# Latent queries by channels for all tokens, later loads of norm constants and residual rows, and other steps for the conditioning map's rows

## Chip, cores and metric

The kernel runs on one core of a Trainium2 chip. The metric is the device time of one execution in microseconds, as the median of several executions. Engines are named as the profile names them: PE (matmul) with PEld (its weight loads), DVE (vector), ACT (scalar), POOL (GpSimd) and SP (the queue that issues most DMAs).

## The reference, cut to what matters

Two layers run over 384 tokens, which are 128 context tokens (block 0) and 256 latent tokens (blocks 1 and 2). Each layer has four token mixers on one combined input projection, a gated merge, an output product with a normalisation, and then an MLP with a second normalisation. All weights and inputs are fp32.

```python
def _layer(x, cond, lp, mixer_fn):
    mod = jax.nn.silu(cond) @ lp['w_ada'] + lp['b_ada']
    sh1, sc1, g1, sh2, sc2, g2 = jnp.split(mod[:, None, :], 6, axis=-1)
    y, extra = mixer_fn(x * (1 + sc1) + sh1)
    x = _layernorm(ALPHA * x + g1 * y, lp['ln1_g'], lp['ln1_b'])
    h = x * (1 + sc2) + sh2
    f = jnp.square(jax.nn.relu(h @ lp['w_up'])) @ lp['w_down']
    x = _layernorm(ALPHA * x + g2 * f, lp['ln2_g'], lp['ln2_b'])
...
    qa = (_rmsnorm(q_lat, lp['mla_q_norm']) @ lp['mla_w_uq']).reshape(b, t, MLA_HEADS, MLA_NOPE + MLA_ROPE)
    return dict(
        a_q_nope=qa[..., :MLA_NOPE], a_q_pe=qa[..., MLA_NOPE:],
        a_ckv=_rmsnorm(kv_lat, lp['mla_kv_norm']), a_k_pe=k_pe,
...
    q_pe = _apply_rope(p['a_q_pe'], cos_a, sin_a)
    k_pe = _apply_rope(p['a_k_pe'][:, :, None, :], cos_a, sin_a)[:, :, 0]
...
    terms = [jax.nn.sigmoid(gates[..., i * D_MODEL:(i + 1) * D_MODEL]) * (o @ lp['w_branch'][i])
             for i, o in enumerate(outs)]
    return (terms[0] + terms[1] + terms[2] + terms[3]) @ lp['w_o']
```

Branch A is latent attention with four heads of 64 channels without position and 32 with position (its query latents have 256 channels). Branch B is retention with a norm per head, C is windowed attention, D is dense attention.

## The kernel before, in words

**Products.** Each fp32 weight tile of 128x1024 is split in two parts that PE can multiply at its fast rate: ACT copies the high part (L283), DVE subtracts for the low part (`split_low`, L127), and every product is three matmuls (`mm3`, L122 to L124). `Stream` holds the order of all weight tiles, loads up to four ahead into a ring of six raw buffers (`raw_load`, L274, on SP's queue) and splits two ahead.

**Order of a layer's first half.** The projection writes the mixers' inputs by token (`tm[key, t]`). After each block of a projection or a gate product the kernel calls `tick()`, which takes one more task into the `Pipe` and runs one stage of every task in it. Layer 0 has 16 ticks in the projections and 32 in the gates (two for each pair of gate columns), layer 1 has 22 and 32. Then `tick()` runs rows of the conditioning map: a call of the generator `ada_vector` is one DVE operation over 128x1024 (L378), and the rows' weights come through the same ring of raw buffers. How many calls a tick makes stands in `TICK_OPS` as pairs of a first tick and a number n; a tick makes n/2 calls, rounded up at odd ticks and down at even ones. Once the attention's buffers are given back (`p2` is set, ahead of the last branch's gates) n is 2. What is left is run by `for _ in ada_v: pass` ahead of the output product. Layer 0 has 48 calls, layer 1 has 32.

**Latent queries (branch A).** `prep_a(t)` makes three stages for each of three token blocks. `norms` takes sums of squares (L790, L791), the inverse root on POOL, two transposes of the query latents (L799) and a DVE copy of them (L800). `up_q` multiplies them with the up weights (L819, output by token, 384 columns, plain fp32), scales by the norm (L824), turns the position keys, and rotates the positional part of the queries on POOL and DVE. `turn` transposes each head's 96 channels back (L837, four transposes for a block) and copies them to `qTA` (L838). `keys_a` and `values_a` follow as tasks of their own, so branch A has five tasks ahead of its attention.

**Retention's norm.** `out_b(t)` has four stages: products, `norm`, `apply` (four DVE operations over 128x64, L1086, and one over 128x256, L1088) and `turn` (two transposes, L1096).

**Output product and normalisation.** `out_product` multiplies 8 (mixer) or 32 (MLP) weight tiles into six PSUM banks, all tokens at once for the first part (`lead`), and then the last `rest` tiles block by block, so that a block's normalisation (`layer_norm`) runs under the next block's matmuls. `raw` multiplies by the gate (L1250), adds the residual (L1251) and takes statistics (L1254). The very last block of the kernel has its second half cut into two pieces of 256 columns. The banks of the output product are those that the branch products used, so its first matmuls wait for the merge (`mid_done`, L1192).

**Late constants.** The norm constants (gate rows from DRAM and the norm's gain and bias, `norm_consts`, L1225, on POOL's queue) and the three residual blocks (`xs`, L1438, on SP's queue) are asked for ahead of the output product. A scheduler orders each engine's instructions by the program's order and its own estimate of when they are ready, so that these loads may move ahead of their place; `behind(later, earlier)` pins one instruction after another in that order.

Of the kernel before, what the change touches and what calls it, by code (L numbers as in the profile page):

```python
# [20 lines left out]
L = 2  # L21
# [20 lines left out]
TICK_OPS = ((4, 2), (14, 1), (29, 4))  # L42
# [53 lines left out]
def kernel(ctx, tc, a):  # L96
# [14 lines left out]
    def nm(s):  # L111
        counter[0] += 1
        return f"{s}_{counter[0]}"
# [157 lines left out]

    def raw_load(src, pool=None, bufs=RAWS):
        raw = raw_tile(src.shape[-1], pool, bufs)
        nc.sync.dma_start(out=raw, in_=src)  # L274
        return raw
# [190 lines left out]
    for l in range(L):  # L466
# [315 lines left out]
        def prep_a(t):  # L782
            st_ = {}
            tok = slice(t * P, (t + 1) * P)
            rs = rsa[:, t]

            def norms():
                x = tm["a", t]
                sq = t2("sq")
                nc.scalar.activation(sq[:, 0:256], x[:, 0:256], AF.Square, accum_out=rs[:, 0:1])  # L790
                nc.scalar.activation(sq[:, 256:384], x[:, 256:384], AF.Square, accum_out=rs[:, 1:2])  # L791
                nc.vector.tensor_scalar(out=rs[:, 0:1], in0=rs[:, 0:1], scalar1=1.0 / 256, scalar2=EPS, op0=ALU.mult,
                                        op1=ALU.add)
                nc.vector.tensor_scalar(out=rs[:, 1:2], in0=rs[:, 1:2], scalar1=1.0 / 128, scalar2=EPS, op0=ALU.mult,
                                        op1=ALU.add)
# [9 lines left out]
                if t == 0:  # L805
                    nc.sync.dma_start(out=a["o_ckv"][0, l], in_=kv)
                    nc.sync.dma_start(out=a["o_kpe"][0, l], in_=x[:, 384:416])
                    st_["pe"] = x[:, 384:416]
                else:
# [3 lines left out]
                    st_["pe"] = r.rearrange("p h s f -> p (h s f)")  # L813

            def up_q():
                qlT = st_["qlT"]
                qb = bank(psa)
# [3 lines left out]
                nc.tensor.transpose(tb[:, 0:P], tm["a", t][:, 256:384], ident)  # L821
# [284 lines left out]
        for t in range(3):  # L1106
            pipe.add(*prep_a(t))
# [616 lines left out]
```

## Time and profile before

| | |
|---|---|
| median of 3 runs | 1275.6 us (1275.33 to 1277.57) |
| the profiled execution | 1278.41 us, of which 1276.3 us are its span |
| busy | PE 1255.7 us, PEld 1140.0, DVE 852.7, ACT 583.5, POOL 214.5 |
| granted TensorE clock, mean | 0.996 |

The span runs from the first to the last instruction. All rows have times from the span's start. Matmuls overlap, so a row's duration is longer than the step from one matmul's start to the next one's; the step is what a matmul costs. A row of a window gives the stretch, its length, the busy time (and instructions) of PE, PEld, DVE, ACT and POOL, PE's granted clock, the DMA engines' mean busy share and GB/s. An entry such as [2.39 <-DVE tt L1192] says that the engine was idle for 2.39 us and what ended it.

### The profile page before, as it was taken

Reading aid. Unit: us, or ns where it says so; the run is one execution under the profiler, and the core shown is the slowest. Engines: PE = TensorE matmul, PEld = TensorE weight load, DVE = VectorE, ACT = ScalarE, POOL = GpSimd, SP = SyncE. Lnnn points to the kernel's source line nnn. Section 1 sums busy time; section 2 is a strip of 40 time slices with the busy share of each in tenths; the row PEclk is TensorE's granted clock in tenths of the full one; section 3 lists DMA queues with packets and bytes.
Section 4 is the critical chain, followed back from the end, with each engine's and each line's share of the span. In section 5 each row is a group of like instructions: output and inputs, shape, how many; then the busy total and the mean of one; then the engine's idle time right before and its main releaser. Section 6 shows DMA issues by size and latency. Waiting matters only on the chain. (4 is left out here: it accounts for less than half of the span.)

```text
span 1276.3 us, 19137 instructions
## 1 busy us (share of the span) xinstructions
PE 1255.7 (98%) x7264; PEld 1140.0 (89%) x7264; DVE 852.7 (67%) x1537; ACT 583.5 (46%) x1054; POOL 214.5 (17%) x218
## 2 busy tenths in 40 slices
PE   9999999999999999999999999999999999999996
PEld 7889888999889999999898988999998999999995
DVE  4676965899679999443486876597456893333345
ACT  4654563333446444454365566233343744444451
POOL 0032200333232000000061210024221500000004
PEclk9999999999999999999999999999999999999998
DMA  9843323469626787454324422348344263334421
GB/s 371 335 153 118 124 87 104 145 207 348 203 84 233 264 275 272 160 166 136 116 84 147 157 92 83 120 151 326 118 149 161 102 216 132 125 123 158 168 71 50
DMA packets 65259, 211.65 MB, mean 166 GB/s; under 512 B 9296, under 2 KB 13840, under 8 KB 65040
## 3 DMA queue, kind: packets, MB, share of 16 engines
q1 hardware_dynamic: 62448, 201.88, 45.1%
q0 software_dynamic: 2432, 8.42, 1.9%
q8 instruction: 57, 0.93, 0.3%
q14 instruction: 34, 0.28, 0.1%
q10 hardware_dynamic: 288, 0.14, 0.0%
HBM read 206.28 MB, written 4.13 MB: 165 GB/s over the span
## 5 line engine op out<-in xcount | busy, mean ns | idle before, releaser
L127 DVE TENSOR_TENSOR wl<-raw,wh 128x1024 fp32r<-128x1024 f32 (+1 forms) x249 | 315.3, 1271 | 291.5 <-ACT wh L283 291.0
L283 ACT CAST wh<-raw 128x1024 fp32r<-128x1024 f32 x247 | 258.3, 1050 | 438.8 <-PE bank L123 285.8
L122 PE MATMUL bank<-hTh,wh 128*128 128x384 f32 x1040 | 351.4, 338 | 0.0
L124 PE MATMUL bank<-hTh,wl 128*128 128x384 f32 x1040 | 348.8, 336 | 0.6 <-DVE wl L127 0.6
L123 PE MATMUL bank<-hTl,wh 128*128 128x384 f32 x1040 | 348.4, 335 | 0.0
L122 PEld LDWEIGHTS bank<-hTh,wh 128*128 128x128 f32 x1040 | 195.3, 188 | 4.7 <-issue 1.9
L123 PEld LDWEIGHTS bank<-hTl,wh 128*128 128x128 f32 x1040 | 195.3, 188 | 3.1 <-issue 0.9
L124 PEld LDWEIGHTS bank<-hTh,wl 128*128 128x128 f32 x1040 | 195.2, 188 | 1.2 <-DVE wl L127 0.9
L123 PE MATMUL bank<-wl,uh 128*128 128x512 f32 (+1 forms) x376 | 146.5, 390 | 0.1
L124 PE MATMUL bank<-wh,ul 128*128 128x512 f32 (+1 forms) x376 | 146.3, 390 | 0.0
L122 PE MATMUL bank<-wh,uh 128*128 128x512 f32 (+1 forms) x376 | 145.7, 387 | 0.0
L378 DVE CUSTOM_DVE_ANT_0 acc<-raw,csr,bT 128x1024 bf16<-128x1024 f32 x80 | 105.0, 1327 | 1.7 <-POOL rope L766 0.9
L1193 POOL TENSOR_TENSOR tt<-tt,tt 128x384 f32<-128x384 f32 x48 | 65.5, 1384 | 207.7 <-DVE tt L1192 207.6
L378 DVE CUSTOM_DVE_ANT_0 acc<-lnc,csr,bT 128x1024 bf16<-128x1024 f32 x80 | 100.3, 1288 | 0.0
L124 PEld LDWEIGHTS bank<-wh,ul 128*128 128x128 f32 x376 | 70.4, 188 | 14.8 <-DVE ul L127 0.4
L123 PEld LDWEIGHTS bank<-wl,uh 128*128 128x128 f32 x376 | 70.6, 188 | 13.9 <-DVE wl L127 0.6
L122 PEld LDWEIGHTS bank<-wh,uh 128*128 128x128 f32 x376 | 70.7, 188 | 13.3
L122 PE MATMUL bank<-wh,hTh 128*128 128x256 f32 x240 | 71.7, 299 | 0.2 <-ACT tmc L644 0.2
L124 PE MATMUL bank<-wh,hTl 128*128 128x256 f32 x240 | 68.7, 286 | 0.0
L123 PE MATMUL bank<-wl,hTh 128*128 128x256 f32 x240 | 68.3, 285 | 0.0
L399 POOL DMA_DIRECT2D gd<-gs x4 | 2.4, 595 | 290.5 <-DMA raw<-in_w_u_dram 158.0
L710 ACT ACTIVATE p<-bank,neg 128x384 f32<-128x384 f32 (+1 forms) x72 | 35.9, 509 | 30.1 <-DVE neg L707 16.2
(280 smaller groups left out, 1857.8 us busy)
## 6 DMA issues: line engine op xcount, KB each, us to landing
raw<-in_w_g_dram SPq DMA_DIRECT2D x64, 512.0 KB, 3.5
raw<-in_w_d_dram SPq DMA_DIRECT2D x62, 512.0 KB, 3.5
raw<-in_w_u_dram SPq DMA_DIRECT2D x58, 512.0 KB, 3.6
raw<-in_w_av_dram SPq DMA_DIRECT2D x40, 512.0 KB, 3.7
lnc<-in_w_av_dram SPq DMA_DIRECT2D x40, 512.0 KB, 4.3
raw<-in_w_q_dram SPq DMA_DIRECT2D x28, 512.0 KB, 3.7
raw<-in_w_ada_dram SPq DMA_DIRECT2D x16, 512.0 KB, 8.4
raw<-in_w_b_dram SPq DMA_DIRECT2D x16, 512.0 KB, 3.5
```

The source lines that it names most:

```text
L122: mm(out, lhsT=a_hl[0], rhs=b_hl[0], start=start, stop=False)
L123: mm(out, lhsT=a_hl[0], rhs=b_hl[1], start=False, stop=False)
L124: mm(out, lhsT=a_hl[1], rhs=b_hl[0], start=False, stop=stop)
L127: nc.vector.tensor_tensor(out=low, in0=x, in1=high.bitcast(F32), op=ALU.subtract)
L283: nc.scalar.copy(wh, raw)
L378: nc.vector.tensor_tensor_reduce(out=alloc().bitcast(BF16), in0=w, in1=csr[:, c], scale=1.0, scalar=bT[:, l, u, b:b + 1], op0=ALU.mult, op ...
L399: nc.gpsimd.dma_start(out=g_dram[l][w].rearrange("c (k p) -> (c k) p", p=P), in_=gs)
L710: nc.scalar.activation(p[:, j, c], ss[j][:, c], AF.Exp, bias=neg[:, i, j:j + 1], scale=scale, accum_out=su[:, i, j:j + 1])
L1193: nc.gpsimd.tensor_tensor(out=acc[c], in0=acc[c], in1=t_, op=ALU.add)
```

## The change

- **Latent queries.** Blocks are normalised in place (`norms_a`, query latents too), then all 384 tokens are transposed together (`turn_q`), and the up product is made with the weights as the stationary operand for the 256 channels without position (`nope_q`: the output is by channel and needs no transpose). Only the 128 positional channels are made by token (`rope_q`), rotated, and transposed once for a block (`turn_rope`, all heads in one). The up weights are repacked to match. Branch A has seven tasks ahead of its attention instead of five.
- **Norm constants and residual rows.** They are issued by `step_wo(k)` within the output product of the mixer half: the constants at k = 1 behind POOL's last instruction, the residual blocks at k = 1, 2, 3 behind the last weight load issued so far.
- **Map's rows.** `TICK_OPS` changes from ((4, 2), (14, 1), (29, 4)) to ((4, 2), (14, 1), (21, 4), (28, 1)).
- **Retention's norm.** `apply` runs on ACT with a bias made by one more DVE operation.
- **Last block.** It isn't cut into 256 columns any more; its statistics are two pieces as for the others.

```diff
-TICK_OPS = ((4, 2), (14, 1), (29, 4))
+TICK_OPS = ((4, 2), (14, 1), (21, 4), (28, 1))
...
+    loaded = []
+
     def raw_load(src, pool=None, bufs=RAWS):
         raw = raw_tile(src.shape[-1], pool, bufs)
         nc.sync.dma_start(out=raw, in_=src)
+        loaded.append(nc.cur_bb.bb.instructions[-1])
         return raw
...
+        def norms_a(t):
+
+            def f():
+                rs, x = rsa[:, t], tm["a", t]
+                sq = small([P, 256], "tanh", 1)
+                nc.scalar.activation(sq, x[:, 0:256], AF.Square, accum_out=rs[:, 0:1])
+                nc.scalar.activation(sq[:, 0:128], x[:, 256:384], AF.Square, accum_out=rs[:, 1:2])
...
                 rsqrt(rs, rs, 2)
-                tb = bank(psm)
-                for k in range(2):
-                    nc.tensor.transpose(tb[:, k * P:(k + 1) * P], x[:, k * P:(k + 1) * P], ident)
-                nc.vector.tensor_copy(sq[:, 0:256], tb[:, 0:256])
-                st_["qlT"] = sq
+                nc.scalar.mul(x[:, 0:256], x[:, 0:256], rs[:, 0:1])
                 kv = x[:, 256:384]
...
-                for k in range(2):
-                    mm(qb[:, :384], lhsT=qlT[:, k * P:(k + 1) * P], rhs=wq[:, k], start=(k == 0), stop=(k == 1))
...
+        def turn_q():
+            pa["q"] = []
+            for k in range(2):
+                tb = bank(psm)
+                for t in range(3):
+                    nc.tensor.transpose(tb[:, t * P:(t + 1) * P], tm["a", t][:, k * P:(k + 1) * P], ident)
+                q = t2("qlT")[:, :NTOK]
+                (nc.scalar.copy if k else nc.vector.tensor_copy)(q, tb[:, :NTOK])
+                pa["q"].append(q)
...
+        def rope_q():
+
+            b = bank(psm)
+            for t in range(3):
+                tok = slice(t * P, (t + 1) * P)
                 for k in range(2):
-            def turn():
-                tb = bank(psm)
-                for h in range(4):
-                    nc.tensor.transpose(tb[:96, h * P:(h + 1) * P], st_["q"][:, h * 96:(h + 1) * 96], ident)
-                nc.scalar.copy(qTA[:96, :, tok], tb[:96].rearrange("p (h n) -> p h n", h=4))
+                    mm(b[:, tok], lhsT=pa["q"][k][:, tok], rhs=wq[:, k, 256:384], start=(k == 0), stop=(k == 1))
+            r = pa["r"] = t2("ropeq")
+            nc.vector.tensor_copy(r[:, :NTOK], b[:, :NTOK])
...
+        def nope_q():
+            for i in range(2):
+                b = bank(psa)
+                for k in range(2):
+                    mm(b[:, :NTOK], lhsT=wq[:, k, i * P:(i + 1) * P], rhs=pa["q"][k], start=(k == 0), stop=(k == 1))
+                nc.scalar.copy(qTA[0:64, 2 * i, :], b[0:64, :NTOK])
+                (nc.scalar.copy if i else nc.vector.tensor_copy)(qTA[0:64, 2 * i + 1, :], b[64:128, :NTOK])
+
+        def turn_rope():
+            tb = bank(psm)
+            for t in range(3):
+                nc.tensor.transpose(tb[:, t * P:(t + 1) * P], pa["rq", t] if t else pa["r"][:, 0:P], ident)
...
+                nb = small([P, 4], "nbb", 1)
+                nc.vector.scalar_tensor_tensor(out=nb, in0=mv[:, :, 0], scalar=-1.0, in1=rs, op0=ALU.mult, op1=ALU.mult)
...
-                    nc.vector.tensor_scalar(out=oh, in0=oh, scalar1=mv[:, h, 0:1], scalar2=rs[:, h:h + 1],
-                                            op0=ALU.subtract, op1=ALU.mult)
+                    nc.scalar.activation(oh, oh, AF.Identity, bias=nb[:, h:h + 1], scale=rs[:, h:h + 1])
...
         for t in range(3):
-            pipe.add(*prep_a(t))
-        pipe.add(keys_a)
-        pipe.add(values_a)
+            pipe.add(norms_a(t))
+        pipe.add(turn_q)
+        pipe.add(lambda: (rope_q(), turn_kv()), turn_rope)
+        pipe.add(nope_q)
+        pipe.add(lambda: (keys_a(), values_a()))
...
-                for i in range(c0 // size, c1 // size):
-                    nc.vector.bn_stats(st[:, i], src[h][:, i * size - 512 * h:(i + 1) * size - 512 * h])
+                nc.vector.bn_stats(st[:, h], src[h][:, c])
...
-                    last_part(2, cuts=(0, 512, 768, 1024))
-                    sums(2, cuts=(0, 512, 768, 1024))
+                    last_part(2)
+                    sums(2)
...
-        c1 = norm_consts(0)
         mod2 = modulation(l, 1, (l, 0))
-        xs = []
-        for t in range(3):
-            xt = p2.tile([P, D], F32, tag="x", name=nm("x"), bufs=3)
-            nc.sync.dma_start(out=xt, in_=a["x_tm"][t] if l == 0 else x_dram[t])
-            xs.append(xt)
+        c1, xs = [], []
+
+        def step_wo(k):
+            if k == 1:
+                mark, n = last_issued()[mybir.EngineType.Pool], len(nc.cur_bb.bb.instructions)
+                c1.extend(norm_consts(0))
+                for i in nc.cur_bb.bb.instructions[n:]:
+                    if i.engine == mybir.EngineType.Pool:
+                        behind(i, mark)
+            if k in (1, 2, 3):
+                xt = p2.tile([P, D], F32, tag="x", name=nm("x"), bufs=3)
+                nc.sync.dma_start(out=xt, in_=a["x_tm"][k - 1] if l == 0 else x_dram[k - 1])
+                behind(nc.cur_bb.bb.instructions[-1], loaded[-1])
+                xs.append(xt)
+
...
-                    first_up, between=first_evac)
+                    first_up, step_wo, first_evac)
```

## Rows read from the trace of the kernel before

**Rows 1.** The page, parts 1 and 6.

```profile
PE 1255.7 (98%) x7264; PEld 1140.0 (89%) x7264; DVE 852.7 (67%) x1537; ACT 583.5 (46%) x1054; POOL 214.5 (17%) x218
...
raw<-in_w_g_dram SPq DMA_DIRECT2D x64, 512.0 KB, 3.5
```

**Rows 2.** Windows of layer 0: engines' busy time, clock, DMA share, GB/s.

```profile
169.00:190.30 21.30, 21.22 (x138) 18.39 (x137) 12.42 (x29) 14.03 (x42) 0.00 (x0) 1.00 0.22 75
190.30:216.20 25.90, 25.52 (x181) 22.62 (x180) 13.37 (x24) 10.54 (x20) 2.04 (x2) 1.00 0.32 107
256.30:316.00 59.70, 58.23 (x337) 57.78 (x337) 59.35 (x82) 19.57 (x28) 20.82 (x17) 1.00 0.77 278
316.00:338.00 22.00, 22.00 (x127) 21.64 (x125) 15.32 (x24) 11.03 (x19) 4.95 (x4) 1.00 0.60 204
338.00:362.00 24.00, 21.61 (x89) 17.53 (x88) 12.31 (x12) 8.23 (x10) 2.95 (x2) 0.93 0.56 179
```

**Rows 3.** The same windows for line L378 alone: DVE busy.

```profile
256.30:316.00 59.70, 31.02 (x47) 1.00 0.77 278
```

**Rows 4.** Timeline, layer 0, at the start of the mixer's output product.

```profile
334.97 0.83 ACT L283 CAST o<-raw 128x768 fp32r<-128x768 f32 x1 [6.43 <-DMA raw<-in_w_u_dram]
...
340.08 1.01 DVE L1192 SCALAR_TENSOR_TENSOR tt<-tt,bank 128x384 f32<-128x384 f32 x2
...
340.68 0.80 PE L122 MATMUL bank<-wh,mh 128*128 128x512 f32 x1 [2.39 <-DVE tt L1192]
```

**Rows 5.** Timeline, layer 1, at the same place.

```profile
956.98 0.84 ACT L283 CAST o<-raw 128x768 fp32r<-128x768 f32 x1 [4.76 <-DMA raw<-in_w_u_dram]
...
963.47 0.40 PE L123 MATMUL bank<-wl,mh 128*128 128x512 f32 x1
963.70 0.40 PE L124 MATMUL bank<-wh,ml 128*128 128x512 f32 x1
964.01 0.49 PE L122 MATMUL bank<-wh,mh 128*128 128x512 f32 x1
```

**Rows 6.** DMA view of 285 to 318 us: issues, KB each, median us to landing.

```profile
raw<-in_w_g_dram SPq DMA_DIRECT2D x7, 512.0 KB, 7.3
...
x<-in_x_tm_dram SPq DMA_DIRECT2D x3, 512.0 KB, 8.9
```

**Rows 7.** Timeline of PE, layer 0: latent queries.

```profile
61.74 0.64 PE L837 MATMUL bank<-ident,qA 128*96 128x128 f32 x4
...
68.30 0.59 PE L819 MATMUL bank<-wmla,sq 128*128 128x384 f32 x1 [0.44 <-DVE sq L800]
```

**Rows 8.** Timeline, waits around retention's norm, layers 0 and 1.

```profile
258.95 2.10 DVE L1086 TENSOR_SCALAR oB<-oB,mv,rsb 128x64 f32<-128x64 f32 x4
...
260.96 1.27 DVE L378 CUSTOM_DVE_ANT_0 acc<-raw,csr,bT 128x1024 bf16<-128x1024 f32 x1
...
262.73 0.41 PE L1096 MATMUL bank<-ident,oB 128*128 128x128 f32 x2 [1.47 <-DVE oB L1088]
...
857.92 0.41 PE L1096 MATMUL bank<-ident,oB 128*128 128x128 f32 x2 [0.34 <-DVE oB L1088]
...
869.88 0.44 PE L124 MATMUL bank<-hTh,wl 128*128 128x384 f32 x1 [0.62 <-DVE wl L127]
```

**Rows 9.** Timeline, end of the kernel: second halves of its last two blocks.

```profile
1258.17 0.70 DVE L1250 TENSOR_TENSOR bank<-bank,lnc 128x512 f32<-128x512 f32 x1 [1.92 <-PE bank L124]
...
1260.36 0.21 DVE L1257 BATCH_NORM_AGGREGATE lnmv<-lnst 128x2 f32<-128x12 f32 x1
...
1266.12 0.28 PE L123 MATMUL bank<-o,uh 128*128 128x256 f32 x1
1266.24 0.28 PE L124 MATMUL bank<-o,ul 128*128 128x256 f32 x1
...
1266.56 0.43 DVE L1250 TENSOR_TENSOR bank<-bank,lnc 128x256 f32<-128x256 f32 x1 [2.09 <-PE bank L124]
...
1269.42 0.26 DVE L1257 BATCH_NORM_AGGREGATE lnmv<-lnst 128x2 f32<-128x24 f32 x1
```

More of the change, by code (lines that the diff above doesn't have):

```diff
@@ L807, in norms @@
                     nc.sync.dma_start(out=a["o_kpe"][0, l], in_=x[:, 384:416])
-                    st_["pe"] = x[:, 384:416]
+                    pa["pe", t] = x[:, 384:416]
                 else:
@@ L834, in turn @@
-            def turn():
-                tb = bank(psm)
-                for h in range(4):
-                    nc.tensor.transpose(tb[:96, h * P:(h + 1) * P], st_["q"][:, h * 96:(h + 1) * 96], ident)
-                nc.scalar.copy(qTA[:96, :, tok], tb[:96].rearrange("p (h n) -> p h n", h=4))
-            return norms, up_q, turn
+                    pa["pe", t] = r.rearrange("p h s f -> p (h s f)")
+            return f
+        def turn_q():
[7 more added lines that the diff above has]
+                pa["q"].append(q)
@@ new lines, in turn_kv @@
+        def turn_kv():
+            tb = bank(psa)
+            for t in range(3):
+                nc.tensor.transpose(tb[:, t * P:(t + 1) * P], tm["a", t][:, 256:384], ident)
+            nc.vector.tensor_copy(ckvT[:, :NTOK], tb[:, :NTOK])
+            tb = bank(psa)
+            for t in range(3):
+                nc.tensor.transpose(tb[:32, t * P:(t + 1) * P], pa["pe", t], ident)
+            nc.scalar.copy(kTA[64:96, :, :NTOK], tb[0:32, :NTOK].unsqueeze(1).to_broadcast([32, 4, NTOK]))
+        def rope_q():
+            b = bank(psm)
+            for t in range(3):
+                tok = slice(t * P, (t + 1) * P)
+                for k in range(2):
+                    mm(b[:, tok], lhsT=pa["q"][k][:, tok], rhs=wq[:, k, 256:384], start=(k == 0), stop=(k == 1))
+            r = pa["r"] = t2("ropeq")
+            nc.vector.tensor_copy(r[:, :NTOK], b[:, :NTOK])
+            for t in (1, 2):
+                qv = r[:, t * P:(t + 1) * P].rearrange("p (h s f) -> p h s f", h=4, s=2)
+                if t == 1:
+                    rq = r[:, NTOK:].rearrange("p (h s f) -> p h s f", h=4, s=2)
+                else:
+                    rq = small([P, 4, 2, 16], "rqo", 1)
+                rope(rq, qv, cos_a[:, t - 1, 0:16], sin_a[:, t - 1, 0:16], 16)()
+                pa["rq", t] = rq.rearrange("p h s f -> p (h s f)")
@@ new lines, in nope_q @@
+        def nope_q():
[7 more added lines that the diff above has]
+            tb = bank(psm)
+            for t in range(3):
+                nc.tensor.transpose(tb[:, t * P:(t + 1) * P], pa["rq", t] if t else pa["r"][:, 0:P], ident)
+            for h in range(4):
+                (nc.vector.tensor_copy if h == 0 else nc.scalar.copy)(qTA[64:96, h, :],
+                                                                      tb[32 * h:32 * h + 32, :NTOK])
@@ L1236, in layer_norm @@
             gb, lg_, lb_ = consts[cnd], consts[2], consts[3]
-            st = p2.tile([P, 4, 6], F32, tag="lnst", name=nm("lnst"), bufs=2)
-            st = st if mod is None and t == 2 else st[:, 0:2]
-            size = D // st.shape[1]
+            st = p2.tile([P, 2, 6], F32, tag="lnst", name=nm("lnst"), bufs=2)
             mv = p2.tile([P, 2], F32, tag="lnmv", name=nm("lnmv"), bufs=2)
@@ L1660, in _pack @@
     wm = np.zeros((L, P, 1280), f)
-    wm[:, :, 0:768] = v["mla_w_uq"].reshape(L, 2, P, 384).transpose(0, 2, 1, 3).reshape(L, P, 768)
+    uq = v["mla_w_uq"].reshape(L, 2, P, 4, 96)
+    uq = np.concatenate([uq[..., :64].reshape(L, 2, P, 256), uq[..., 64:].reshape(L, 2, P, 128)], -1)
+    wm[:, :, 0:768] = uq.transpose(0, 2, 1, 3).reshape(L, P, 768)
     wm[:, :, 768:1024] = v["mla_w_uk"]
```

36 lines of the change are left out of this document (6 added, 30 removed).

## Prediction

> **What bounds the kernel now.** I read the page first. PE is busy for 98% of the span, no other engine for more than 67% outside its weight loads [rows 1], so a gain must come from fewer matmuls, from stretches in which PE waits, or from the tail after the last matmul. The windows then show where PE has no cover: from 256.3 to 316 us DVE is busy for 59.35 of 59.70 us and the DMA engines for 77% [rows 2], and 31.02 us of DVE's time are rows of the map alone [rows 3]. Right behind this, where the output product of layer 0 begins, PE stands still for 2.39 us [rows 4] and the window that holds this has a mean granted clock of 0.93, while the other windows have 1.00 [rows 2]. The reader is to see a backlog: DVE full, then late weights, then an idle PE, then a low clock.
>
> How the wait comes about: ACT stands for 6.43 us in front of a cast whose weights have not landed, the merge on DVE (L1192) runs only at 340.08, and PE's first matmul needs the bank that the merge reads [rows 4]. In layer 1 ACT waits for the same kind of load for 4.76 us, but at 956.98, some 6.5 us ahead of the matmul at 963.47, and there PE takes 0.31 us for one step, where 0.23 us is the normal one [rows 5]. In layer 0 the same cast comes at 334.97, only 5.7 us ahead of 340.68. So the difference between the layers is how late the stream of weights is.
>
> **The change part by part.**
>
> *Fewer transposes.* Before, four transposes for each of three blocks and two layers turn the queries back, 24 in all; after, three a layer, 6. Four of them span 0.64 us and one lasts 0.27 us as the 0.28 us matmuls beside it do, so a step is about (0.64 - 0.28) / 3 = 0.12 us [rows 7]. 18 x 0.12 = 2.2 us of PE. The up product itself keeps its columns (2304 for a layer, in 384 and 128 wide pieces), so I price it at nothing, with 0.5 us to either side for the shorter pieces. "TensorE: Matmul & The Clock Gate" of the Trainium skill (part 4, PE-mode transpose) gives about 275 ns for one 128x128 transpose inside a kernel. By that figure the gain would be an estimated 18 x 0.275 = 5.0 us; the trace agrees with it as a duration, but not as a cost, since the steps are 0.12 us.
>
> *The waits of the latent path.* PE waits 0.44 us for a DVE copy of the latents [rows 7]; such waits are few. The new path chains more (norm, scale in place, transpose, copy, product, rotation, transpose) and spreads it over seven ticks, with projections as cover; attention begins two ticks later, and its last stage moves from tick 34 to 36, while the output buffers are taken at tick 40. I take no change, and bound it by three such waits to either side, 1.3 us.
>
> *Map's rows.* By the rule of the ticks layer 0 makes 10 calls in ticks 4 to 13 in both kernels. Before: 7 in ticks 14 to 28, 24 in ticks 29 to 40, 7 more after. After: 3 in ticks 14 to 20, 14 in ticks 21 to 27, 6 in ticks 28 to 40, 8 in ticks 41 to 48, and 7 left for the drain ahead of the output product. A call lasts 1.27 us [rows 8]. So ticks 21 to 27, about 169 to 216 us, get 14 x 1.27 = 17.8 us more. DVE is busy there for 12.42 + 13.37 of 47.2 us [rows 2], so it would be at 43.6, or 92%. PE may then wait for attention steps behind a row. The nearest rows of such a wait are 0.34 to 1.47 us with DVE full [rows 8]; below, it is nothing, since the mean has room. I take 1.0 us lost, and 4 us (three of the longer ones) as the upper end.
>
> *Where the rows leave.* DVE loses 18 calls from ticks 29 to 40, 22.9 us. Three waits stand in stretches where DVE had rows of the map between the steps that PE needs: 1.47 us and 0.34 us for retention's norm, and 0.62 us for a split low part [rows 8]. In the first a map row of 1.27 us stands between the norm's two operations. I count all three: 2.4 us. The 7 calls left for the drain find DVE free for 6.7 us from 316 to 338 us and for 11.7 us after [rows 2]; I price them at nothing, and their other end is the slower rival's. Moving `apply` to ACT takes 2.10 us from this full DVE and gives it to ACT, busy for 19.57 of 59.70 us [rows 2]. "ScalarE: Activation LUTs" of the Trainium skill (what ACT_TABLE_LOAD costs) states that each per-partition operand adds about 93 ns to an activation. By that page's figures four of them would last an estimated 1.4 us, so the move alone gains little; no row of the kernel before shows this shape on ACT.
>
> *Norm constants and residual rows.* The three residual blocks, 512 KB each, were loaded between 285 and 318 us; a weight load then takes 7.3 us to land and a residual block 8.9 us [rows 6], against 3.5 us for the same weight loads over the whole kernel [rows 1]. After, the constants (four loads on POOL) are issued behind POOL's last merge, which follows the DVE merge at 340.08 [rows 4], so at about 344 us. They are needed when block 0 is done, near 360 us by the pace of PE: 16 us against 8.9 us, so I cost them at nothing; without that cover they would cost what exceeds it. The residual blocks now queue on SP among the last weight loads for the output product, ahead of just the loads for which ACT waits. Each takes 512 KB at the 278 GB/s of the busy window [rows 2], 1.9 us, and two can stand in front. Layer 1 has slack there [rows 5], so I take 0.5 us for both layers, from 0 to 3.8 us.
>
> *The wait at the output product.* With DVE and the DMA engines relieved ahead of it, the stream should be as early as in layer 1, and layer 0's wait goes: 2.39 us of idle PE, and the clock. A mean of 0.93 over 24 us [rows 2] means 24 x 0.07 = 1.7 us lost, which is 3.4 us at 1.2 in place of 2.4 GHz after that idle time. Together 4.1 us. Next to be late would be what layer 1 shows, about 0.1 us.
>
> *The last block.* The first 256-column piece starts on DVE only at 1266.56, after the last matmul of the bank (1266.24), though its own columns were done earlier [rows 9]: the cut hides nothing. It takes 1269.42 - 1266.56 = 2.86 us to the aggregation; the uncut block before takes 1260.36 - 1258.17 = 2.19 us. That saves 0.7 us of the end path. On PE, 18 matmuls of 512 columns at 0.23 us [rows 5] replace 36 of 256 at 0.12 us [rows 9]: 0.2 us.
>
> The sum: -2.2 - 0.2 (matmuls), -0.7 (tail), -2.4 (waits near the map's rows), -4.1 (output product), +1.0 (rows in attention), +0.5 (residual rows) = -8.1 us. It is made against the profiled execution, 1278.4 us with 2.1 us outside the span; the median of the runs is 2.8 us lower, so I take the difference from the median: 1275.6 - 8.1 = 1267.5 us.
>
> **The rivals.**
>
> *The wait stays (0.18).* ACT's wait is for a load, and layer 1, with no full DVE ahead of it, has it too for 4.76 us [rows 5]. If the residual rows keep these loads late in layer 0, nothing of the 4.1 us comes: 1275.6 - 4.0 = 1271.6 us. Against it speaks that the same wait in layer 1 costs PE nearly nothing.
>
> *Attention becomes DVE's bound (0.12).* Ticks 21 to 27 hold D's attention and retention, which also move two ticks later; DVE was light there [rows 2], which speaks against it. At the upper end, 4 us in place of 1.0: 1270.5 us. With the first rival too (0.05): 1274.6 us.
>
> *The rows left over stand at the output product (0.10), slower.* The drain holds 7 calls, 7 x 1.27 = 8.9 us of DVE. DVE is busy for 15.32 of 22 us just ahead and for 12.31 of 24 us behind [rows 2]; with these calls and those of the last ticks it would be full from 316 us on. If the scheduler puts them ahead of the merge that frees PE's first bank, PE waits up to 8.9 us in place of 2.39, with the clock's 1.7 us as before. The output product then loses 6.5 us in place of gaining 4.1: 1275.6 - 4.0 + 6.5 = 1278.1 us, and slower still where late splits follow. The point from which it decides: beyond 5 calls ahead of the merge the other gains are eaten. For it speaks that the calls precede the output product in the program; against it, that before the rows ran ahead of their ticks whenever DVE was free.
>
> **How the numbers follow.** The forecast has 0.55: 1267.5 us. Its own bounds run from 1264 us (no loss in attention or from the residual rows, latent waits gained) to about 1271 us. The range goes to 1273.6 us, which takes in the first two rivals with 2 us for the residual rows; outside are the two rivals together, the slower one, and little below, some 0.17. A measurement of this kernel can tell 0.2%, or 2.6 us, from no change: faster is below 1273.0 us. The forecast gives 0.53 of faster, the first rival 0.14, the second 0.09: 0.76. Of the slower rival 0.08 lies beyond 1278.2 us. The rest, 0.16, is the same.
>
> **What would show it.** Right: 6 transposes for the queries' positional part and none of 96 channels; DVE well under full from 256 to 316 us; the wait at the output product under 0.5 us in both layers and no lowered clock there; the uncut block's 2.2 us at the end; the constants landing before 360 us. Wrong: a PE idle of over 2 us at either output product, map rows between the last merge operations, several new waits of PE for DVE from 169 to 230 us, or a residual row landing after its block's product.

## The result and the profile after

The changed kernel takes 1283.26 us in the median of four runs (1281.75 to 1284.43), beside 1275.88 us for the kernel before on the same chip: a ratio of 1.0060, with an interval of 1.0048 to 1.0072. It is 7.4 us slower, where 8.1 us less were forecast. The profiled execution took 1281.75 us, with a span of 1279.6 us: 3.3 us over the profiled execution of before. The medians lie 7.4 apart because the run profiled before was 2.5 above its median of 1275.88 and the one profiled after is 1.5 below its own. The traces therefore explain 3.3 us, and the experiments have to say what the rest is. The other three executions of the changed kernel had a mean granted clock of 0.992 to 0.994, the profiled one 0.996, so by this figure they spent more time at the lower clock than the trace shows. Two executions among the experiments, of 3193.89 us (e3) and 2506.39 us (e13), are left out of the ratios, not of the medians.

The page, part 1, of the changed kernel: busy time, share of the span and instructions.

```profile
PE 1255.5 (98%) x7244; PEld 1141.0 (89%) x7244; DVE 842.7 (66%) x1509; ACT 592.0 (46%) x1082; POOL 204.2 (16%) x218
```

Nothing in this line shows a loss; PE is as busy as before [rows 1], with a longer span. The windows show it. First the kernel before, with the columns of [rows 2], in five stretches. The prediction had looked at a part of the attention (130 to 220 us) [rows 2] and at two waits of the last stretch [rows 8]:

```profile
0.00:25.00 25.00, 23.67 (x153) 17.39 (x154) 10.02 (x29) 10.00 (x20) 0.56 (x6) 1.00 0.94 362
56.00:70.00 14.00, 13.56 (x94) 11.48 (x93) 8.27 (x26) 8.78 (x24) 3.17 (x7) 1.00 0.63 210
130.00:220.00 90.00, 87.98 (x588) 77.39 (x585) 66.92 (x167) 48.16 (x116) 9.01 (x8) 1.00 0.33 110
664.00:676.00 12.00, 12.00 (x89) 10.60 (x87) 6.66 (x26) 7.00 (x21) 2.96 (x7) 1.00 0.82 258
850.00:900.00 50.00, 49.04 (x284) 48.40 (x283) 35.90 (x52) 17.12 (x24) 18.02 (x15) 1.00 0.72 263
```

Then the changed kernel, with most windows of [rows 2] among them:

```profile
0.00:25.00 25.00, 22.30 (x146) 16.10 (x147) 9.65 (x26) 10.00 (x19) 0.56 (x6) 1.00 0.95 356
56.00:70.00 14.00, 10.69 (x76) 10.22 (x75) 7.85 (x17) 7.81 (x19) 1.81 (x3) 0.88 0.58 201
130.00:220.00 90.00, 88.03 (x581) 77.29 (x581) 77.96 (x194) 50.59 (x128) 18.53 (x18) 1.00 0.40 134
169.00:190.30 21.30, 20.32 (x141) 18.01 (x140) 20.95 (x62) 9.91 (x23) 0.72 (x1) 1.00 0.58 194
190.30:216.20 25.90, 25.90 (x166) 22.19 (x165) 22.86 (x57) 18.79 (x53) 2.02 (x2) 1.00 0.41 136
256.30:316.00 59.70, 59.70 (x351) 59.60 (x350) 47.70 (x88) 23.27 (x39) 16.92 (x14) 1.00 0.57 185
338.00:362.00 24.00, 21.97 (x104) 18.63 (x103) 14.26 (x20) 10.69 (x14) 6.28 (x7) 1.00 0.87 307
664.00:676.00 12.00, 9.91 (x70) 9.70 (x70) 6.53 (x21) 5.94 (x20) 6.10 (x8) 0.86 0.64 235
850.00:900.00 50.00, 50.00 (x295) 49.90 (x294) 29.90 (x66) 18.84 (x34) 13.02 (x12) 1.00 0.40 137
```

How to read them: a window's length less PE's busy time is idle time, and the length times what the clock lacks of 1.00 is what the low clock cost.

- 56 to 70 us (layer 0, projections): 3.31 idle and 14 x 0.12 = 1.7 of clock, against 0.44 before: **+4.6**.
- 664 to 676 us (layer 1, the same place): 2.09 idle and 12 x 0.14 = 1.7, against nothing: **+3.8**.
- 338 to 362 us (entry of layer 0's output product): 2.03 idle at full clock, against 2.39 and 1.7: **-2.1**.
- 256 to 316 and 850 to 900 us (retention's norm and the late split): 0 in place of 1.47 and 0.96: **-2.4**.
- 130 to 220 us (attention): 1.97 idle in place of 2.02: **nothing**. The 0.98 from 169 to 190 us is a wait that stands at 154.77 in the kernel before, outside that window.
- 0 to 25 us, which no edit touches (the first weight loads land later in this execution): **+1.4**.

That is +5.3. Over the whole span PE's idle time between its first and last matmul grew from 9.7 to 13.8 us, and there are two stretches of half clock in place of one (1.7 us more): +5.8, so that some 0.5 lies in smaller waits (the largest 0.59 us at 88.5). PE's busy time, which holds the steps and what the half clock adds to them, fell from 1255.7 to 1255.5 us; with 1.7 more of half clock in it, the steps themselves fell by about 1.9. The tail behind the last matmul is 0.65 us shorter. Together 5.8 - 1.9 - 0.65 = 3.25 of the 3.3 us. So the gains came, and two new stalls of PE and their clock ate them.

**What PE waits for.** The first stall on PE in layer 0 and in layer 1 (timeline; the lines behind each show the step from start to start, 0.12 us where the clock is still full and 0.21 where it is lowered):

```profile
62.25 0.39 PE L122 MATMUL bank<-wh,hTh 128*128 128x256 f32 x1 [2.89 <-ACT tmd L647]
62.48 0.28 PE L123 MATMUL bank<-wl,hTh 128*128 128x256 f32 x1
62.60 0.28 PE L124 MATMUL bank<-wh,hTl 128*128 128x256 f32 x1
...
671.35 0.58 PE L122 MATMUL bank<-wh,hTh 128*128 128x256 f32 x1 [2.09 <-ACT tmc L647]
671.73 0.42 PE L123 MATMUL bank<-wl,hTh 128*128 128x256 f32 x1
671.94 0.41 PE L124 MATMUL bank<-wh,hTl 128*128 128x256 f32 x1
```

Both wait for an evacuation on ACT (L647 copies a projection's PSUM bank to SBUF). ACT's own timeline says why the evacuation is late. First the kernel before at this place in layer 0 and in layer 1 (there ACT waits for PE), then the changed one in both:

```profile
52.87 1.70 ACT L233 ACTIVATE acc<-csr 128x512 f32<-128x512 f32 x3
54.76 0.63 ACT L233 ACTIVATE acc<-csr 128x512 f32<-128x512 f32 x1 [0.18 <-DVE csr L235]
56.08 0.38 ACT L644 COPY tmd<-bank 128x256 f32<-128x256 f32 x1 [0.69 <-DVE csr L235]
...
666.44 0.37 ACT L644 COPY tmc<-bank 128x256 f32<-128x256 f32 x1 [2.02 <-PE bank L124]
```

```profile
54.26 0.46 ACT L792 ACTIVATE tanh<-tma 128x256 f32<-128x256 f32 x1
...
56.45 0.51 ACT L798 ACTIVATE tma<-tma,rsa 128x256 f32<-128x256 f32 x1 [0.66 <-POOL rsa L190]
...
58.25 0.51 ACT L798 ACTIVATE tma<-tma,rsa 128x256 f32<-128x256 f32 x1 [1.00 <-POOL rsa L190]
58.67 1.66 ACT L233 ACTIVATE acc<-csr 128x512 f32<-128x512 f32 x3
60.50 0.63 ACT L233 ACTIVATE acc<-csr 128x512 f32<-128x512 f32 x1 [0.18 <-DVE csr L235]
61.83 0.37 ACT L647 COPY tmd<-bank 128x256 f32<-128x256 f32 x1 [0.69 <-DVE csr L235]
...
668.73 0.51 ACT L798 ACTIVATE tma<-tma,rsa 128x256 f32<-128x256 f32 x1 [1.70 <-POOL rsa L190]
...
670.53 0.51 ACT L798 ACTIVATE tma<-tma,rsa 128x256 f32<-128x256 f32 x1 [1.00 <-POOL rsa L190]
670.94 0.35 ACT L647 COPY tmc<-bank 128x256 f32<-128x256 f32 x1
```

The scaling of the query latents in place (L798) needs POOL's inverse root, and ACT stands for it: 1.66 us in layer 0 and 2.70 in layer 1 ahead of the evacuation. In layer 0 a second thing stands there: the four tanh pieces of the condition rows (L233, in `cond_rows`). They ran in the kernel before too, but from 52.87 and ahead of the squares; now the squares and two scalings come first, the pieces run from 58.67, and the first evacuation of D's projection comes at 61.83 in place of 56.08.

**What became of the map's rows.** DVE in front of layer 0's output product (timeline; L381 is a map row):

```profile
329.27 1.28 DVE L381 CUSTOM_DVE_ANT_0 acc<-raw,csr,bT 128x1024 bf16<-128x1024 f32 x1
...
330.48 1.28 DVE L381 CUSTOM_DVE_ANT_0 acc<-raw,csr,bT 128x1024 bf16<-128x1024 f32 x1
...
331.68 1.28 DVE L381 CUSTOM_DVE_ANT_0 acc<-raw,csr,bT 128x1024 bf16<-128x1024 f32 x1
...
336.98 1.28 DVE L381 CUSTOM_DVE_ANT_0 acc<-raw,csr,bT 128x1024 bf16<-128x1024 f32 x1
...
344.67 1.01 DVE L1220 SCALAR_TENSOR_TENSOR tt<-tt,bank 128x384 f32<-128x384 f32 x2
...
345.27 0.51 PE L122 MATMUL bank<-wh,mh 128*128 128x512 f32 x1 [2.03 <-DVE tt L1220]
```

The last four rows ahead of the output product, which by the tick rule belong to the drain, stand among splits and earlier merges ahead of the last merge (L1220), for which PE's first matmul of the output product waits 2.03 us. This is the place of [rows 4].

**Other parts answer as forecast.** The positional queries are turned by three transposes (L862), and the last block is uncut; its end on DVE answers to [rows 9]:

```profile
77.77 0.38 PE L862 MATMUL bank<-ident,ropeq 128*128 128x128 f32 x2
78.07 0.33 PE L862 MATMUL bank<-ident,rqo 128*128 128x128 f32 x1
...
1270.52 0.70 DVE L1276 TENSOR_TENSOR bank<-bank,lnc 128x512 f32<-128x512 f32 x1 [1.92 <-PE bank L124]
...
1272.78 0.21 DVE L1282 BATCH_NORM_AGGREGATE lnmv<-lnst 128x2 f32<-128x12 f32 x1
```

### The profile page after: what moved, and what is told of

Same layout as the page of the kernel before. It is cut to its first block, busy times and chain, and to the rows that moved or that the text cites. A ratio compares the mean times of both kernels' runs of the same rounds, so it can differ in the third digit from the quotient of the medians.

```text
span 1279.6 us, 19068 instructions
## 1 busy us (share of the span) xinstructions
PE 1255.5 (98%) x7244; PEld 1141.0 (89%) x7244; DVE 842.7 (66%) x1509; ACT 592.0 (46%) x1082; POOL 204.2 (16%) x218
## 5 line engine op out<-in xcount | busy, mean ns | idle before, releaser
L123 PE MATMUL bank<-wl,uh 128*128 128x512 f32 x372 | 145.8, 392 | 0.1
L124 PE MATMUL bank<-wh,ul 128*128 128x512 f32 x372 | 145.7, 392 | 0.0
L122 PE MATMUL bank<-wh,uh 128*128 128x512 f32 x372 | 145.0, 390 | 0.0
L381 DVE CUSTOM_DVE_ANT_0 acc<-raw,csr,bT 128x1024 bf16<-128x1024 f32 x80 | 102.1, 1289 | 7.0 <-DMA raw<-in_w_av_dram 6.9
L381 DVE CUSTOM_DVE_ANT_0 acc<-lnc,csr,bT 128x1024 bf16<-128x1024 f32 x80 | 100.3, 1288 | 0.0
L1221 POOL TENSOR_TENSOR tt<-tt,tt 128x384 f32<-128x384 f32 x48 | 59.7, 1257 | 191.7 <-DVE tt L1220 191.5
L122 PEld LDWEIGHTS bank<-wh,hTh 128*128 128x128 f32 x240 | 47.4, 197 | 8.2 <-ACT tmd L647 3.1
```

The source lines that it names most:

```text
L122: mm(out, lhsT=a_hl[0], rhs=b_hl[0], start=start, stop=False)
L123: mm(out, lhsT=a_hl[0], rhs=b_hl[1], start=False, stop=False)
L124: mm(out, lhsT=a_hl[1], rhs=b_hl[0], start=False, stop=stop)
L381: nc.vector.tensor_tensor_reduce(out=alloc().bitcast(BF16), in0=w, in1=csr[:, c], scale=1.0, scalar=bT[:, l, u, b:b + 1], op0=ALU.mult, op ...
L1221: nc.gpsimd.tensor_tensor(out=acc[c], in0=acc[c], in1=t_, op=ALU.add)
```

## The experiments

Each is timed beside the kernel before, whose median was 1275.5 to 1275.7 in all four batches. "Latent path" is the new `norms_a` to `turn_rope` with its packing.

**e1: the latent path alone**, on the kernel before.

```diff
-            pipe.add(*prep_a(t))
-        pipe.add(keys_a)
-        pipe.add(values_a)
+            pipe.add(norms_a(t))
+        pipe.add(turn_q)
...
```

> The kernel before with the new path of the latent queries alone. Theory (the scaling of the latents on ACT waits for POOL's root, the evacuations of the projection stand behind it on ACT, PE waits for its bank, and the clock falls): about 1280 us, 4 us slower than before, with idle PE of 2 to 3 us behind an evacuation (tmd, tmc) near 60 us and near 670 us, and a lowered clock in both places, against 18 transposes fewer (2.2 us). Rival (the map's rows in other steps, or the later loads, make the loss): no slower than before, 1273 to 1276 us.

Measured: 1287.05 us, ratio 1.0088 (1.0073 to 1.0103). The path alone loses 11.4 us, more than the whole change and far more than the 4 us expected. PE waits 2.9 us for tmd and 2.0 for tmc, each with half clock behind it, and the wait of 2.2 us at the entry of the output product, with its half clock, is still there. Its profiled span is 11.0 us longer; tmd, tmc and their clock are 8.4 of it, and the rest is spread over smaller waits, among them 1.4 us for retention's norm in layer 1 (0.3 before) and 1.0 in attention (0.5 before).

**e2: the whole change without the latent path.**

```diff
-            pipe.add(norms_a(t))
+            pipe.add(*prep_a(t))
...
```

> The kernel after with the old path of the latent queries. Theory (the latent path makes the loss): 1270 to 1274 us, faster than before, with no idle PE of over 1 us from 50 to 75 us and from 660 to 685 us. Rival (rows of the map, or later loads): 1278 us or more.

Measured: 1272.91 us, 0.9979 (0.9970 to 0.9988). The other edits gain 2.7 us; the path costs 1283.3 - 1272.9 = 10.4 us beside them.

**e3: the ticks alone**, on the kernel before.

```diff
-TICK_OPS = ((4, 2), (14, 1), (29, 4))
+TICK_OPS = ((4, 2), (14, 1), (21, 4), (28, 1))
```

> The kernel before with the new steps of the map's rows alone. Theory (latent path): within 2 us of before; the wait of 1.5 us for retention's norm in layer 0 goes, some waits in attention come. Rival (rows in the attention stretch, or the seven left over, make the loss): 1279 us or more, with rows of the map in front of the merge at the first output product.

Measured: 1276.60 us, 1.0009 (0.9999 to 1.0018): no change that can be told. Retention's wait is gone from its trace. The wait at the output product is 2.7 us with half clock behind it, where the profiled execution of before has 2.39, and two waits for retention's scores (atts) make 1.5 us in place of 0.4. The profiled execution, at 1276.39, is 2.0 us under that of before; in the medians nothing of this is left.

**e4: the later loads alone**, on the kernel before.

```diff
-        c1 = norm_consts(0)
...
+        def step_wo(k):
+            if k == 1:
...
+                c1.extend(norm_consts(0))
```

> The kernel before with the norm constants and residual rows loaded within the output product, alone. Theory (latent path): 1272 to 1276 us; the wait at the first output product may stay, at about 2 us. Rival (the later loads collide with the weights): 1279 us or more, with an idle PE of over 2.4 us at an output product.

Measured: 1274.85 us, 0.9993 (0.9985 to 1.0002). In its trace the stretch from 338 to 362 us has no idle time and a full clock, where the kernel before has 2.39 and 0.93 [rows 2]:

```profile
338.00:362.00 24.00, 24.00 (x108) 19.64 (x107) 13.56 (x16) 7.05 (x8) 5.17 (x6) 1.00 0.76 272
```

So the stall that was forecast to go is not in this trace, and the median gains 0.8 us only. The executions of the kernel before point to why: of the 90 in the four batches, five had a mean granted clock of 0.996, as the profiled one had, and took 1278.14 to 1279.24 us; the other 85 had 0.997 or 0.998, and none took more than 1277.57. The profiled execution, at 1278.41, belongs with the five. Most executions of the kernel before can't have paid its 4.1 us in full.

**e5: the changed kernel with the scaling on DVE.**

```diff
-                nc.scalar.mul(x[:, 0:256], x[:, 0:256], rs[:, 0:1])
+                nc.vector.tensor_scalar(out=x[:, 0:256], in0=x[:, 0:256], scalar1=rs[:, 0:1], scalar2=None,
+                                        op0=ALU.mult)
```

> The kernel after with the latents' scaling by the norm on DVE in place of ACT. Theory (ACT's queue stands at the scaling, which waits for POOL's root, with the projection's evacuations behind it): the idle PE of 2 to 3 us behind tmd and tmc goes in both layers or falls under 1 us, with the lowered clock; about 1275 us, 7 us or more under the kernel after. Rival (the new path is too long a chain wherever the scaling runs, or its evacuations on ACT are too many): over 1280 us with PE still waiting for evacuations near 60 and 670 us.

Measured: 1279.51 us, 1.0032 (1.0020 to 1.0043), 3.75 us better than the changed kernel, between the two expectations. Layer 1's stall is gone from the trace; layer 0's is 2.4 us, still with half clock, and the entry waits 4.0 us. So ACT's wait for the root is layer 1's stall, and not the whole of layer 0's. In layer 0 the wait for POOL now stands in DVE's queue, ahead of the multiplications (L234, L235) for which the fourth tanh piece on ACT waits, and the first evacuation of D's projection comes only at 59.66 (DVE's row, then ACT's):

```profile
56.63 0.35 DVE L798 TENSOR_SCALAR tma<-tma,rsa 128x256 f32<-128x256 f32 x1 [0.82 <-POOL rsa L190]
...
58.34 0.63 ACT L233 ACTIVATE acc<-csr 128x512 f32<-128x512 f32 x1 [1.94 <-DVE csr L235]
```

**e6: the scaling on ACT, one tick later.**

```diff
                 rsqrt(rs, rs, 2)
+
+            def g():
+                rs, x = rsa[:, t], tm["a", t]
                 nc.scalar.mul(x[:, 0:256], x[:, 0:256], rs[:, 0:1])
...
-            pipe.add(norms_a(t))
+            pipe.add(*norms_a(t))
```

> The kernel after with the scaling still on ACT, but as a second stage of each block's task, one tick later than its sums of squares. Theory: the root is done by the time ACT comes to the scaling, so ACT waits less than 0.5 us each time and PE's two waits go: 1274 to 1278 us. Rival (ACT's total work in these ticks, not its wait): no better than the kernel after, 1281 us or more.

Measured: 1281.66 us, 1.0037 (1.0026 to 1.0048), in two groups: three runs from 1276.4 to 1277.3 with a mean clock of 0.996 to 0.998, nine from 1281.2 to 1282.3 (the profiled one among them) with 0.993 or 0.994. Layer 1's wait falls to 0.9 us, layer 0's stays at 2.8: there ACT no longer waits long for the root (0.53 us once), yet tmd comes behind the tanh pieces. The entry waits 4.1 us, with 6.8 us of half clock. The run is inconclusive in time and clear in where ACT stands.

**e7: e5 with the old ticks.**

```diff
-TICK_OPS = ((4, 2), (14, 1), (21, 4), (28, 1))
+TICK_OPS = ((4, 2), (14, 1), (29, 4))
```

> The kernel after with the scaling on DVE and the map's rows in their former steps. If the new steps of the rows help here as in the kernel without the latent path: 2 us slower than with the scaling on DVE alone. If the seven rows left over cost more than the relief from 256 to 316 us gives: 1 to 3 us faster, with the wait at the first output product under 0.5 us.

Measured: 1280.48 us, 1.0033 (1.0020 to 1.0045). That is 1.0 us over e5, the time of neither expectation. The entry's wait falls to 0.7 us (a wait of 1.3 us for ACT stands at 324.1, in the merge before it), but layer 0's stall costs more in this execution: 2.4 us idle and 6.8 us at half clock, a clock of 0.76 in the window from 56 to 70 us.

**e8: everything but the latent path and the ticks** (later loads, `apply` on ACT, uncut end).

```diff
+        def step_wo(k):
...
+                    nc.scalar.activation(oh, oh, AF.Identity, bias=nb[:, h:h + 1], scale=rs[:, h:h + 1])
...
+                    last_part(2)
```

> The kernel before with the later loads, retention's norm on ACT and the uncut last block; old latent path, old steps of the map's rows. If these parts add up: 0.8 us of the loads, 0.9 us of the last block and up to 1.8 us of the waits for retention's norm, 1272 to 1274 us. Rival (the new steps of the rows made the gain of the kernel without the latent path): within 1 us of before.

Measured: 1273.96 us, 0.9988 (0.9979 to 0.9996); 0.9 us better than e4, of which the tail is 0.65.

**e9: e5 with the condition rows spread.** The first tanh piece stays ahead of the D projection, the others follow its three blocks.

```diff
                 nc.vector.tensor_tensor(out=x, in0=x, in1=th, op=ALU.mult)
+                yield
...
-            cond_rows(lambda: t2("acc"))
+            part = cond_rows(lambda: t2("acc"))
+            next(part)
...
-                proj(w, 256, evac_to(key, c0, scale), tick)
+                proj(w, 256, evac_to(key, c0, scale), (lambda: (tick(), next(part))) if l == 0 and key == "d" and c0 == 0 else tick)
```

> The changed kernel with the latents scaled on DVE, and with layer 0's four tanh pieces of the condition rows no longer in one run ahead of the D projection but one ahead of it and one behind each of its three blocks. Theory (ACT's order: sums of squares plus condition rows stand in front of the evacuations for which PE waits): the wait of 2.4 us for tmd at 59 us and the half clock behind it go, 4 us against the run with the scaling on DVE alone (1279.5), so about 1275.5. Rival (the latents' own chain is late, ACT's order matters little): PE waits as long elsewhere between 55 and 70 us, and the time stays within 1 us of 1279.5.

Measured: 1273.56 us, 0.9982 (0.9972 to 0.9992), 6.0 us below e5: the theory's 4 and more. PE has no wait for tmd or tmc over 0.2 us in the trace, and the entry's wait in the profiled execution is 1.7 us. Its runs spread from 1271.0 to 1276.5.

**e10: e9 with the old ticks** (e7's edit).

> The same with the old ticks of the map's rows. Theory: with both causes gone, the new latent path has only its saved transposes (2.2 us) left against the kernel with old latents, old ticks, later loads and uncut end (1273.96): 1272 us, at most 1274 with the waits of about 1 us in attention that the two versions with the new path showed. Rival (the path's later end, two ticks, is what costs): 1277 or more, with the loss spread from 100 to 340 us.

Measured: 1274.59 us, 0.9993 (0.9984 to 1.0001). Neither expectation: 0.6 us above e8, the same kernel with the old path. No stall is left in the projections; PE waits 2.3 us for ACT's exponentials in attention, 1.7 for retention's norm, 1.3 for ACT in the merge, 1.0 for retention's scores. Against e8's trace PE's steps are 2.0 us shorter and its idle time between matmuls is 1.7 us longer (10.6 against 8.9): with the old ticks most of what the fewer transposes save is given back in waits.

**e11: e9 without rows for the drain.**

```diff
-TICK_OPS = ((4, 2), (14, 1), (21, 4), (28, 1))
+TICK_OPS = ((4, 2), (14, 1), (21, 4), (28, 2))
```

> The same with the new ticks, but two operations a tick in place of one from tick 28 on, so that no row of the map is left for the drain. Theory (the left-over rows hold the entry of layer 0's output product): no wait over 1.7 us and no half clock near 340 us, the retention norm's waits partly back; about 1272 us. Rival (the entry's wait comes from the late weight stream or from ACT, not from the rows left over): 2.5 us or more of idle PE at 340 us stay.

Measured: 1269.11 us (1269.03 to 1269.58), 0.9950 (0.9938 to 0.9963). This version beats both kernels, by 6.5 and 14.2 us, and its runs agree within 0.6 us. Its windows where the changed kernel lost:

```profile
56.00:70.00 14.00, 14.00 (x119) 13.82 (x118) 9.95 (x20) 7.44 (x15) 1.40 (x2) 1.00 0.78 246
338.00:362.00 24.00, 24.00 (x108) 19.87 (x107) 13.43 (x19) 4.87 (x6) 4.41 (x7) 1.00 0.68 254
664.00:676.00 12.00, 12.00 (x98) 11.49 (x97) 8.47 (x18) 5.71 (x8) 3.29 (x6) 1.00 0.62 231
```

PE is busy for all of each, at full clock. The longest single waits that are left are 1.2 us at the start and 1.0 in attention (the view of waits: engine, line and releaser, total, times, longest):

```profile
PE bank L732 <- ACT p L721: 1.8, 2, 1.0
PE bank L590 <- DVE zero L491: 1.2, 1, 1.2
```

**e12: e2 without rows for the drain** (e11's edit).

> The changed kernel with the old latent path (1272.9) and no row left for the drain. Theory as in the run before: the 3.2 us of idle PE and the half clock at 341 us go, about 1269 us, with up to 2 us back for retention's norm: 1269 to 1271. Rival: the wait at the entry stays and the time is within 1 us of 1272.9.

Measured: 1272.09 us, 0.9971 (0.9960 to 0.9982). The entry's wait goes from the trace as the theory has it (3.2 us in e2), but the time only moves by 0.8, by the rival's number: e2's profiled execution, at 1276.36, was 3.5 us above its median, so most of its runs did not pay that wait in full. Beside e11 this prices the latent path without its stalls: 1269.1 - 1272.1 = -3.0 us. (e11 alone has the spread condition rows; in the two traces PE's steps differ by 2.0 us.)

**e13: the changed kernel with the condition rows spread alone** (e9's edit, scaling on ACT).

> The changed kernel with only the condition rows' tanh pieces spread over the first blocks; the latents are still scaled on ACT. It tells the two waits of ACT in layer 0 apart. Theory (each stands in front of the tmd evacuations by itself): in layer 0 the wait at tmd shrinks but does not go, since ACT still waits for the root before each scaling, and layer 1's 2 us at tmc stay with their half clock: 1277 to 1280. Rival (the tanh pieces alone were layer 0's stall): layer 0's wait goes wholly, layer 1's stays: about 1276.

Measured: 1281.01 us, 1.0043 (1.0029 to 1.0057). That is 1 us above the expected range. Layer 0's wait is 1.3 us and its clock stays full (rows below); layer 1's stays at 2.1 with half clock. The entry waits 3.7 us, which the expectation did not have.

```profile
58.23 0.39 PE L122 MATMUL bank<-wh,hTh 128*128 128x256 f32 x1 [1.32 <-ACT tmd L648]
...
56.00:70.00 14.00, 12.68 (x105) 12.29 (x104) 8.34 (x17) 8.82 (x19) 1.40 (x2) 1.00 0.76 245
```

**e14: the changed kernel without rows for the drain, alone** (e11's edit).

> The changed kernel with nothing but two operations a tick from tick 28 on, so that no map row is left for the drain. Theory: it gains what this gained with the other two repairs (4.4 us) or less, since the entry's wait in the changed kernel was 2.0 us without a lowered clock in the profiled run: 2 to 4.5 us below 1283.3, so 1279 to 1281; the waits at tmd and tmc stay. Rival (it gained only beside the other repairs): within 1 us of 1283.3.

Measured: 1279.22 us, 1.0031 (1.0020 to 1.0043), 4.0 us better, as the theory said; tmd and tmc wait as in the changed kernel (2.9 and 2.1 us).

**e15: e11 with the norm constants and residual rows loaded where the kernel before loads them.**

```diff
+        c1 = norm_consts(0)
...
-                c1.extend(norm_consts(0))
```

> The best version so far (scaling on DVE, spread condition rows, no map row left; 1269.1) with the norm constants and residual rows loaded where the kernel before loads them. It prices the later loads by themselves where nothing else disturbs the output product. Theory (the late weight stream was one of two causes of the entry's wait): ACT's cast waits again before layer 0's output product, PE stands 1 to 2.5 us, perhaps with the lowered clock: 1270.5 to 1273. Rival (with the map's rows gone from the stretch the loads no longer matter): within 0.7 us of 1269.1.

Measured: 1273.57 us, 0.9984 (0.9975 to 0.9993): 4.5 us over e11, 0.6 above the theory's range. The place was not the expected one. The entry has no idle time in its trace; PE stands earlier, during the gates, for a split's low part that DVE makes late. PE's row first, then DVE's (timeline; L379 is a map row):

```profile
302.39 0.44 PE L124 MATMUL bank<-hTh,wl 128*128 128x384 f32 x1 [3.88 <-DVE wl L127]
...
298.70 1.28 DVE L379 CUSTOM_DVE_ANT_0 acc<-raw,csr,bT 128x1024 bf16<-128x1024 f32 x1 [4.79 <-DMA raw<-in_w_av_dram]
...
299.91 1.28 DVE L379 CUSTOM_DVE_ANT_0 acc<-raw,csr,bT 128x1024 bf16<-128x1024 f32 x1
...
301.11 2.35 DVE L127 TENSOR_TENSOR wl<-raw,wh 128x1024 fp32r<-128x1024 f32 x2
```

DVE itself waits 4.79 us for a map row's weights, and the split stands behind two rows, so that DVE's order passed the delay to PE. In e11 DVE waits 1.23 us at the same point. What is new beside that load are the four constant loads (POOL's queue, from 280.31 us) and the residual blocks (the first at 282.16), each of 512 KB; the DMA engines are at 84% from 285 to 310 us, in e11 at 67%. Which of the two sets of loads delays it was not tried.

## Why the prediction was wrong, point by point

**The waits of the latent path (no change, 1.3 us to either side): this step failed.** The path costs 11.4 us alone (e1) and 10.4 beside the other edits (e2). The prediction took the nearest waits of PE in the old path, 0.44 us, and counted three. The engine that made the wait was not in that count. The step named the chain "norm, scale in place, transpose" but never asked on which engine the scaling runs, what is queued behind it there and who waits for that: ACT, the evacuations, PE. None of the three rivals has it. Shown: the stalls of 2.89 and 2.09 us and their half clock make 8.4 us in the profiled execution, and with both of ACT's burdens removed (e9) the changed kernel gains 9.7 us. Each takes part by itself: the scaling on DVE gives 3.75 us (e5), the spread tanh pieces 2.25 (e13), and layer 0's wait goes from 2.9 to 2.4 and 1.3 us in the two and to nothing in both. The two single gains make 6.0 of the 9.7; the singles' traces show the entry's wait at 4.0 and 3.7 us, where the changed kernel's has 2.03, so part of a single gain is lost again there; why that wait grows in these two and not in e9 (1.7) is not shown. Why the squares overtook the condition rows was not tried; the new code takes its square's buffer from another pool, and that is only argued.

**Fewer transposes (-2.2), uncut block's matmuls (-0.2): right in size.** The matmul steps at full clock fell by about 1.9 us in all, 0.5 less than the two terms. It shows in time only where the waits are cured and the rows are moved: -3.0 from e12 to e11, but +0.6 from e8 to e10.

**The wait at the output product (-4.1): half right.** It is absent from e4's trace, and the later loads are worth 4.5 us in the best version (e15 to e11, by a wait at another place). But the sum took 4.1 us from one profiled execution and the difference from a median that was 2.8 us below it. In the median the gain was 0.8 (e4): by the 90 executions listed there, few pay the term in full. The forecast subtracted a term of the one from the other without asking whether the term was the very 2.8 us between them.

**The seven leftover calls (priced at nothing): wrong.** This is the slower rival's mechanism, and it happened: four rows stand ahead of the merge, and without leftovers the changed kernel gains 4.0 us (e14), e9 4.4 (e11) and e2 0.8 (e12). Its price of 8.9 us of DVE held as an upper end; the point "beyond 5 calls" was set too high, since four already cost the 4.0 us to which the rival put the other gains. It was not what made the kernel slower by itself (e3: no change).

**The waits near map rows (-2.4): right.** 1.47 and 0.96 us in the windows became nothing.

**Rows in attention (+1.0): nothing of it came.** Over 130 to 220 us PE idles as long as before (1.97 us against 2.02). The wait for ACT's exponentials that now stands at 171.51 (0.98 us) stood at 154.77 before (0.50); it is 1.03 us in e1, whose rows are where they were, and 0.48 in e3, which moves the rows alone, so it grew with the latent path. The forecast of 92% of DVE's time for 169 to 216 us measured 43.8 of 47.2, 93%, and that is luck: the map's rows take 12.8 us more there in place of 17.8, and other work takes 5.2 more.

**The tail (-0.7): right**, 0.65; the uncut block took 1272.78 - 1270.52 = 2.26 us to the aggregation where 2.19 was said.

**Constants and residual rows (+0.5): at most that.** The constants were issued at 348.3, later than the 344 said, and took 9.2 to 13.7 us to land, the last behind the 360 us that was named as a sign, but ahead of the first use at 365.31, which waited for PE.

**`apply` on ACT.** Four operations last 1.44 us, in place of 2.10 on DVE [rows 8]:

```profile
263.81 1.44 ACT L1113 ACTIVATE oB<-oB,nbb,rsb 128x64 f32<-128x64 f32 x4 [0.35 <-DVE nbb L1106]
```

The estimate of 1.4 us by "ScalarE: Activation LUTs" of the Trainium skill (what ACT_TABLE_LOAD costs) agrees with this row.

## What to carry to other kernels

When a step moves or is rewritten, list for each engine what stands in its queue behind the new instruction, evacuations of PSUM above all; an operation that waits for another engine's result belongs on an engine with nothing urgent behind it (in e5 the wait moved to DVE and held up layer 0 from there). Rows of background work need a place for the last of them: a schedule that leaves some for the drain puts them ahead of the next stage's first wait. Before a stall in a profiled execution is counted as a gain, compare that execution's time with the median.

## What was not expected of the hardware

- **A wait of 2 us may cost 1.7 more.** After 2.09 and 2.89 us of idle PE, and after 2.44 in e5, the granted clock fell to half (1.2 GHz) for 3.4 us, beginning as work resumed (671.3) or 1.5 us later (63.7, beside the resumption at 62.25), so that a 256-column step took 0.21 in place of 0.12 us. After 2.05 us in e1 it fell too; after 2.03 us (345.27 us), 1.74 us (e9) and 1.32 us (e13) it stayed full. In e7 2.4 us of idle were followed by 6.8 us at half clock, twice what e5 shows after the same idle time. So the cost of one stall differs between kernels by more than its length.
- **The terms don't add.** The three repairs give 3.75, 2.25 and 4.0 us one by one, 10.0 in all, and 14.2 together.
